# A gated window and dilated attention block: the units' stage keeps projections and attention alone; merges, gating of y and 19 half gate pairs go behind it

## The chip, the cores and the metric

The kernel runs on one core of one Trainium2 chip, as one launch. The metric is device time in microseconds, less is better. The five engines are PE (TensorE, matmul), DVE (VectorE), ACT (ScalarE), POOL (GpSimd) and SP (SyncE, which here issues every DMA). The line numbers L... are those of the kernel before, unless "after" is said.

## What is computed

x is 2048 tokens by 1024 columns. One layer:

```python
h = rms_norm(x, norm_gain)
qa, ka, va, qb, kb, vb, ga, gb, mg = split(h @ w_in)
ya = banded_attention(norm(qa) * s, norm(ka), va, 128, 1, bias, sink) * silu(ga)
for g, (window, dilation) in enumerate(((128, 1), (512, 4), (2048, 16))):
    o, l = dilated_group(norm(qb[g]) * s, norm(kb[g]), vb[g], window, dilation, bias)
yb = sum(softmax(l over the groups) * o) * silu(gb)
gates = sigmoid(mg + b_merge)
x + (gates[0] * (ya @ w_branch_a) + gates[1] * (yb @ w_branch_b)) @ w_out
```

Mixer A has 8 query and 2 key heads of 64, mixer B 8 heads in each of three groups. The gate columns are ga and gb (512 each) and mg (2 x 1024): with 128 columns to a chunk, 8 chunks of ga and gb, and 16 of mg.

## The kernel before

**Precision.** Each operand of a large matmul is split into two f16 parts, hi and lo. A product is three matmuls of a 128 x 128 stationary tile, hi hi, hi lo and lo hi. XH and XL hold the normed x, turned, as f16 parts: 8 chunks of 128 channels by 2048 tokens and 256 more that repeat the first.

**Order.** Every instruction is put out by a planner written by hand: `at(t, f)` puts a step in a heap, `until(t)` puts out those that are due (L390, L396). The times only set the order of the instructions on each engine's own queue; semaphores do the rest. All engines take their queue in order. SP's queue holds all DMAs, also those that wait for data.

**Stages.** (1) x is loaded, normed, turned and split, and the gate chunks 0 and 1 are computed for the four quarters of 512 tokens. (2) The units' stage: 14 units (2 of A, 12 of B, that is four pairs of heads in three groups), each of 8 slots. A slot projects two blocks of 128 tokens to q, k and v (`Pair`, L634): matmul, copy out, norm, split, and a DMA transpose that gives kq, the f16 parts of q and k turned. `Item` (L749) is one block of queries for two heads: logits `s` on PE (L805), maxima on DVE (L820), exp on ACT (L828), split into `p` (ACT L833, DVE L837), a DMA transpose to `pt` (L843), the product with v on PE (L854). An A slot has four items of up to 384 keys, a B slot two of up to 256. For B with dilation 1 or 4 (8 "shifted" units) the key blocks stand half a block off the query blocks, and so q was projected from aligned tokens and k and v from shifted ones: L651 makes 24 matmuls of 128 columns and 24 of 256 there, and 24 of 384 in the other units.

The outputs of A and of group 0 of B stay in SBUF; those of groups 1 and 2 go to DRAM (`zd`, L889) and come back (`zz`, L863). `a_merge` and `b_merge_q` (L945, L978) apply the softmax denominators, in the units' stage. `YPart` (L893) loads a gate chunk (`gtd`), turns y on PE (L916, four transposes each, 32 times), multiplies on DVE (L920), takes the maximum (L925) and stores y to `ytd`. Forty gate steps (`g_step`, L357: 24 matmuls of 512 columns, then tanh on ACT, the gate on DVE, a store) are put into the slots that the table FILLS names (L103), 36 of them in the 112 slots and 4 just behind. Eight more steps (`mg_step`, L1055) follow while the last attention drains.

(3) The gates' stage: the other five pairs of merge chunks. `gate_pair` (L1285) is two steps. `gate_group` (L1382) computes a gate pair for two quarters of the tokens by seven products of half the size in place of eight: 7 x 12 matmuls of 512 columns stand for four steps of 24. It needs sums and differences of blocks of x (`x_sums`, L1328, on DVE and ACT) and of weights (`w_sums`, L1353, on DVE and ACT). Weight pairs are loaded, multiplied by the norm gain on POOL (L180), scaled and split (`prep`, L1305). Before it uses seven products for quarters 0 and 2 of each pair, and steps for quarters 1 and 3.

(4) The branches' stage, `branch_pair` (L1542): y times the branch weights, times the gates; the blocks of the merged result (`a_blocks`, L1497) go to DRAM. (5) The output's stage, `group` (L1618), in seven products for each block.

Of the kernel before, what the change touches and what calls it, by code (L numbers as in the profile page):

```python
# [43 lines left out]
DCS = (3, 1, 5, 0, 4, 2)  # L44
# [16 lines left out]
NPAIR = 8 * NU  # L61

# [7 lines left out]
B_LAST = 0.763  # L70
DRAIN = 0.8
A_MERGE = (0.085, 0.258, 0.51, 0.671, 1.503, 0.761)
B_MERGE = (-0.037, 0.133, 0.333, 0.507, 0.665, 1.053)
Y_PART = (-0.097, 0.483, 0.709, 0.893, 0.943)
GATE = (-0.123, -0.064, 0.329)
W_STEP = (0.1, 0.465, 1.9, 0.445, 4.197, 0.146, 0.342)
W_MAX = (3.762, 3.892)
G_PREP = (5.907, 6.882, 7.102, 7.671, 7.712, 7.812, 7.942)
N_PREP = (6.3, 7.15, 7.753)
B_GAP = (0.25, 0.138, 0.231)  # L80
Y_MAX = (0.026, 0.815, 0.839)
# [8 lines left out]
T_Y = (2.0, 0.8, 1.6, 1.5, 4.0, 26.0, 0.5, 1.3, 2.1, 1.6, 2.0)  # L90
T_P = ((0, 0.0, 0.03), (1, 3.0, 50.0), (2, 56.0, 75.0), (3, 82.0, 102.0), (4, 108.5, 128.3))
T_O = ((0, 62.0, 84.0), (1, 136.4, 154.0), (2, 136.9, 164.6), (3, 183.9, 190.0))
T_G = (143.4, 174.8, 176.0, 177.4)
T_S = (2.0, 11.0, 0.85, 1.6, 0.75, 1.5, 0.9, 1.3, 0.8)
T_H = (157.4, 2.0, 0.02)
T_GATE = (0.1, 0.1, 0.9, 1.0, 1.0)
T_W = (0.3, 5.5, 1.1, 8.5, 0.9, 14.0, 14.7, 16.2, 0.9, 0.8)
T_B = (20.0, 6.5, 1.55, 0.8)
T_BR = (7.0, 0.95, 20.0, 9.0, 34.0)
T_A = (0.3, 0.2, 1.5, 0.8, 1.2)  # L100
T_M = (16.0, 14.0, 2.0, 2.0, 1.0)
# [10 lines left out]
def block_kernel(tc, x, w_units, w_gate, w_mrg, w_brn, w_out, w_bra, gain, qkg, sink, bias_a, bias_b, b_merge, out):  # L112
# [98 lines left out]

    def w_square(u, i):
        raw = wtiles[u][0]
        if i == 0:
            wtiles[u] += [wp.tile([128, NCH, 384], F16, name="wh"), wp.tile([128, NCH, 384], F16, name="wl"),
                          sm.tile([128, 4], F32, name="wsq")]
        n = 384 if u < NU else 256
        c = slice(2 * i, 2 * i + 2)
        A.activation(wtiles[u][2][:, c, :n], raw[:, c, :n], AF.Square, accum_out=wtiles[u][3][:, i:i + 1])
# [12 lines left out]
    def w_hi(u, i):  # L232
        n = 384 if u < NU else 256
        raw, s, inv, wh, wl = wtiles[u]
        c = slice(2 * i, 2 * i + 2)
        A.activation(wh[:, c, :n], raw[:, c, :n], AF.Copy, scale=s[:])
# [43 lines left out]
    zd = [dr.tile([2, S, 132], F32, name=f"zd{p}") for p in range(4)]  # L280
# [32 lines left out]
    gw = {}  # L313
# [12 lines left out]
    def g_square(c):  # L326
        pool = gp if c > 1 else sp0
        bufs = 1 if c > 1 else 2
        gh = pool.tile([128, NCH, 128], F16, name="gh", bufs=bufs)
        gl = pool.tile([128, NCH, 128], F16, name="gl", bufs=bufs)  # L330
# [10 lines left out]
    def g_pow(c):  # L341
# [4 lines left out]
        gw[c] = (gh, gl, ih, raw, s)  # L346

# [190 lines left out]
    for c in range(3):  # L538
        b = X_G[c]
        if c == 2:  # L540
            at(X_G[0] + X_GP[5] + .1, g_load, c)
# [39 lines left out]
    class Unit:  # L581


        def __init__(self, u):
# [13 lines left out]
            self.v, self.kq, self.t, self.done = {}, {}, {}, {}  # L598
            if self.kind == "A" or self.g == 0:
                self.nm = us.tile([128, NT, self.nq], F32, name=f"nm{self.kind}", bufs=2)  # L600
# [33 lines left out]
    class Pair:  # L634
# [7 lines left out]
        def matmuls(self, i):  # L642
# [3 lines left out]
            for a, b, aligned in ((0, 128, True), (128, 384, False)) if un.shift else ((0, 384, True),):  # L646
                h, lo = subset(0, un.g, r, c, aligned), subset(1, un.g, r, c, aligned)
                k = 0
                for ch in range(NCH):
                    for lhs, rhs in ((h, un.wh), (h, un.wl), (lo, un.wh)):  # L650
                        out.append(lambda lhs=lhs, rhs=rhs, ch=ch, a=a, b=b, k=k: T.matmul(  # L651
                            ps[:, a:b], lhsT=lhs[:, ch, :], rhs=rhs[:, ch, a:b], start=(k == 0), stop=(k == 23)))
                        k += 1
# [85 lines left out]
        def turn(self):  # L739
            for i, s in enumerate(self.subsets):  # L740
                if self.un.shift and s[1] == 0:
                    kq = wk.tile([128, 6, 128], F16, name="kq0", bufs=3)
                else:
                    kq = wk.tile([128, 6, 128], F16, name="kq", bufs=KQ_BUFS)
                nc.sync.dma_start_transpose(out=kq[:], in_=self.sp[:, i].rearrange("p a b c -> p (a b c)"))
                self.un.kq[s] = kq


    class Item:  # L749
        def __init__(self, un, r, i, h0):  # L750
# [3 lines left out]
            if un.kind == "A":  # L754
                cs = [c for c in (i - 1, i, i + 1) if 0 <= c < n]
                self.keys = [((0, c), 0, 128) for c in cs]
                self.b0 = 128 * (cs[0] - i + 1)
            elif n == 1:
                cs = [0]
                self.keys = [((r, 0), 0, 128)]  # L760
                self.b0 = 64
            else:
                cs = [i, (i + 1) % n]
                self.keys = [((r, i), 0 if i else 64, 128), ((r, (i + 1) % n), 0, 128 if i + 1 < n else 64)]
                self.b0 = self.p0 = 0 if i else 64
            self.segs = [(r, c) for c in cs]
            self.W = sum(b - a for _, a, b in self.keys)
            self.width = 128 * len(cs)

        def plan(self, s):  # L770
# [5 lines left out]
            if un.kind == "B" and un.g == 0 and self.i % 2 == 0:  # L776
                at(v - .05, self.z_load)
# [12 lines left out]
        def logits(self):  # L790
            un = self.un
            q = un.kq[(self.r, self.i)]
# [954 lines left out]
```

## Time and profile before

| what | us |
|---|---|
| median of 3 runs | 1961.19 (1960.42 to 1961.2) |
| span of the profiled execution, first to last instruction | 1958.6 |
| time around the span, median less span | 2.6 |
| stage 1, x and two gate chunks | 0 to about 70 |
| stages 2 and the drain, units | 70 to about 1466 |
| stage 3, gates | 1466 to about 1604 |
| stage 4, branches | 1604 to about 1810 |
| stage 5, output | 1810 to 1959 |

The profile records no time of its own for the profiled execution outside the span; the 2.6 us are taken as the same for both kernels. A matmul's row has a latency of which most lies beside the next matmul; what PE pays for it is the distance from its start to the next start. On DVE and POOL, too, the next instruction starts before the last has ended, by about 0.08 and 0.01 us. The ends of the stages are read from the chain of work that ended last.

### The profile page before, as it was taken

Reading aid. Unit: us, or ns where it says so; the run is one execution under the profiler, and the core shown is the slowest. Engines: PE = TensorE matmul, PEld = TensorE weight load, DVE = VectorE, ACT = ScalarE, POOL = GpSimd, SP = SyncE. Lnnn points to the kernel's source line nnn. Section 1 sums busy time; section 2 is a strip of 40 time slices with the busy share of each in tenths; the row PEclk is TensorE's granted clock in tenths of the full one; section 3 lists DMA queues with packets and bytes.
Section 4 is the critical chain, followed back from the end, with each engine's and each line's share of the span. In section 5 each row is a group of like instructions: output and inputs, shape, how many; then the busy total and the mean of one; then the engine's idle time right before and its main releaser. Section 6 shows DMA issues by size and latency. Waiting matters only on the chain.

```text
span 1958.6 us, 48091 instructions
## 1 busy us (share of the span) xinstructions
PE 1935.7 (99%) x17606; PEld 1392.0 (71%) x17606; DVE 1377.4 (70%) x3604; ACT 1059.8 (54%) x2415; POOL 956.0 (49%) x2440
## 2 busy tenths in 40 slices
PE   8999999999999999999999999999999999999999
PEld 5567896677788898888989889899544444444444
DVE  6668777888768776667876878767776757876312
ACT  7457656776565566565666655656534545432100
POOL 4254556455546656647566676656511210232533
PEclk8999999999999999999999999999999999999999
DMA  6239987797848596677777776755822346788763
GB/s 250 81 81 168 194 150 159 141 187 141 177 101 184 118 185 126 125 148 164 152 132 154 135 169 126 143 118 118 187 81 85 106 165 195 218 241 268 252 228 145
DMA packets 589773, 308.46 MB, mean 157 GB/s; under 512 B 458080, under 2 KB 527328, under 8 KB 588256
## 3 DMA queue, kind: packets, MB, share of 16 engines
q1 hardware_dynamic: 589536, 305.39, 67.0%
q8 instruction: 137, 2.24, 0.5%
q14 instruction: 100, 0.82, 0.1%
HBM read 129.91 MB, written 65.27 MB: 100 GB/s over the span
## 4 chain that ended last, share of the span: by engine, by line
PE 80%; DVE 6%; POOL 6%; issue 4%; ACT 2%; DMA 2%; SPq 0%; POOLq 0%; DVEq 0%; ACTq 0%
PE pj L651 32%; PE pj L308 14%; PE fps L308 13%; PE fps L1614 7%; PE fps L1409 5%; PE s L805 4%; PE pv L854 4%; POOL rs_t L270 1%; DVE rw L715 1%; POOL rs_t L271 1%; DVE qss L703 1%; POOL rs_t L272 1%; POOL rw L722 1%; POOL rs_y L273 1%; PE pt L916 1%
## 5 line engine op out<-in xcount | busy, mean ns | idle before, releaser
L651 PE MATMUL pj<-wl,XH 128*128 128x128 f16 (+2 forms) x2816 | 715.2, 268 | 0.0
L651 PE MATMUL pj<-wh,XH 128*128 128x128 f16 (+2 forms) x2816 | 708.7, 268 | 4.0 <-DVE vt L691 4.0
L651 PE MATMUL pj<-wh,XL 128*128 128x128 f16 (+2 forms) x2816 | 711.6, 269 | 0.0
L651 PEld LDWEIGHTS <-XH 128*128 128x128 f16 x5632 | 574.6, 113 | 64.7 <-issue 5.8
L651 PEld LDWEIGHTS <-XL 128*128 128x128 f16 x2816 | 318.1, 113 | 26.7 <-issue 0.5
L820 DVE CUSTOM_DVE_ANT_0 pr<-s,b,ubuf 128x256 f32<-128x256 f32 (+3 forms) x512 | 218.6, 464 | 48.6 <-PE s L805 47.0
L270 POOL TENSOR_TENSOR rs_t<-rs_y 128x8 f32<-128x8 f32 (+2 forms) x345 | 105.4, 306 | 207.5 <-DVE rs_y L261 142.7
L837 DVE SCALAR_TENSOR_TENSOR p<-pr,p 128x512 f16<-128x512 f32 (+2 forms) x256 | 185.0, 723 | 21.6 <-ACT p L833 21.1
L308 PEld LDWEIGHTS <-wh 128*128 128x128 f16 x960 | 93.7, 98 | 111.0 <-issue 1.5
L715 DVE TENSOR_TENSOR rw<-rw,qr 128x512 f32<-128x512 f32 (+1 forms) x112 | 111.6, 997 | 86.7 <-POOL vt L678 58.4
L722 POOL TENSOR_TENSOR rw<-rw,g 128x128 f32<-128x128 f32 (+1 forms) x224 | 131.1, 605 | 78.1 <-DVE rw L715 62.1
L833 ACT ACTIVATE p<-pr 128x512 f16<-128x512 f32 (+2 forms) x256 | 159.5, 623 | 7.1 <-issue 0.3
L670 ACT ACTIVATE rw<-pj 128x256 f32<-128x256 f32 (+1 forms) x224 | 86.5, 386 | 134.3 <-PE pj L651 133.4
L737 POOL COPY spl<-spl 128x256 f16<-128x256 f16 (+1 forms) x224 | 93.7, 448 | 127.2 <-DVE spl L732 125.7
L308 PE MATMUL fps<-Y,wh 128*128 128x512 f16 x512 | 152.2, 379 | 0.0
L805 PE MATMUL s<-kq 128*128 128x128 f16 (+1 forms) x1856 | 147.3, 218 | 1.5 <-DMA kq<-spl 1.4
L805 PEld LDWEIGHTS <-kq 128*128 128x128 f16 x2016 | 129.8, 98 | 25.1 <-issue 2.0
L308 PE MATMUL pj<-XH,gh 128*128 128x512 f16 x384 | 145.5, 379 | 0.0
L308 PE MATMUL pj<-XH,gl 128*128 128x512 f16 x384 | 145.5, 379 | 0.0
L308 PE MATMUL pj<-XL,gh 128*128 128x512 f16 x384 | 145.5, 379 | 0.0
L1614 PE MATMUL fps<-wt,M 128*128 128x512 f16 (+1 forms) x684 | 145.2, 375 | 0.0
L728 ACT ACTIVATE spl<-rw 128x512 f16<-128x512 f32 (+1 forms) x112 | 72.1, 644 | 126.2 <-POOL vt L678 87.0
(241 smaller groups left out, 3702.2 us busy)
## 6 DMA issues: line engine op xcount, KB each, us to landing
wraw<-in_w_units_dram SPq DMA_DIRECT2D x56, 384.0 KB, 4.6
mtd<-mm SPq DMA_DIRECT2D x56, 256.0 KB, 3.7
M<-mtd SPq DMA_DIRECT2D x8, 1792.0 KB, 9.5
mgd<-fg SPq DMA_DIRECT2D x39, 256.0 KB, 2.1
zd<-z SPq DMA_DIRECT2D x128, 66.0 KB, 1.9
zz<-zd SPq DMA_DIRECT2D x64, 132.0 KB, 2.9
xt<-in_x_dram SPq DMA_DIRECT2D x16, 512.0 KB, 8.9
gtd<-yo SPq DMA_DIRECT2D x32, 256.0 KB, 2.7
```

Source lines behind the costliest of these rows:

```text
L270: G.tensor_tensor(tv, yv, yv, OP.mult)
L308: out.append(lambda w=w, xx=xx, ch=ch, i=i: T.matmul(ps[:], lhsT=w[:, ch, c0:c0 + 128], rhs=xx[:, ch, ts], start=(i == 0), stop=(i == n - 1)))
L651: out.append(lambda lhs=lhs, rhs=rhs, ch=ch, a=a, b=b, k=k: T.matmul(ps[:, a:b], lhsT=lhs[:, ch, :], rhs=rhs[:, ch, a:b], start=(k == 0), ...
L715: V.tensor_tensor(q, q, self.rr[:, :n].unsqueeze(2).to_broadcast([128, n, HD]), OP.mult)
L722: G.tensor_tensor(q[:, i, :un.nq, :], q[:, i, :un.nq, :], g, OP.mult)
L737: G.tensor_copy(sp[:, i, nh:, :, :], sp[:, i, nq:nh, ::-1, :])
L805: T.matmul(self.sv[j][:, o:o + k1 - k0], lhsT=q[:, h, :], rhs=kt[:, un.nq + kh + v * un.nk, k0:k1], start=(v == 0), stop=(v == 1))
L820: V.tensor_tensor_reduce(out=self.pv[:, j, self.p0:self.p0 + W], in0=self.sv[j], in1=un.bias[:, self.h0 + j, self.b0:self.b0 + W], scale=I ...
L833: A.activation(self.sp[:, :128 * n], self.pr, AF.Copy, scale=PSC)
L837: V.scalar_tensor_tensor(self.sp[:, 128 * n:], self.pr, PSC, self.sp[:, :128 * n], OP.mult, OP.subtract)
L1409: mm.append(lambda ch=ch, k=k, w=w, i=i: T.matmul(ps[:], lhsT=weight(bl, ch)[w], rhs=xblock(x, ch)[k], start=(i == 0), stop=(i == 11)))
L1614: mm.append(lambda ch=ch, k=k, w=w, i=i: T.matmul(ps[:, :cols.stop - cols.start], lhsT=m[:, a, ch, k, :], rhs=wt[w][:, b, ch, cols], start ...
```

## The change

Gate chunks 2 to 7 become three pairs ("s", 2), ("s", 4), ("s", 6), beside the eight merge pairs ("m", ...): 11 pairs of 256 columns. The first runs in eight steps while the attention drains, the second for quarters 1 and 3 in steps, and all else in seven products: 19 halves (a half is a gate pair for two quarters). FILLS is gone, and with it all gate work in the 112 slots. `gate_out` (after L1346) does the tanh and, for "s" pairs, the gate on DVE.

`Pair.matmuls` takes q, k and v from one set of shifted tokens: 24 matmuls of 384 columns for all units. The DMA transposes write into tiles of 512 token columns in token order, at half a block's offset; where a tile begins, a block goes over in two transposes of 64 tokens. `Item.operands` takes q and keys from these tiles, so that a key stretch of up to 256 columns is one matmul.

Every item stores its output to DRAM (`za`, `zd`). `a_merge` runs 8 times and `b_merge_q` 16 times (it was 32, of half the size) in the gates' stage, from DRAM, as does `YPart`; the scales that hang on the maxima of y (`y_scales`) are computed after that. The four sums `whole` in `x_sums` and the four differences in `w_sums` move from DVE to POOL; `x_sums` runs for both pairs of quarters. The splits of the output weights' columns 2 and 3 move into the branches' stage.

```diff
@@ PAIRS
+PAIRS = [("m", dc) for dc in DCS]
+PAIRS[2:2], PAIRS[0:0] = [("s", 4), ("s", 6)], [("s", 2)]
-FILLS = ((2, None, (2, 2, 4, 5)), (3, 0, (8, 9, 10, 12)), (4, 1, (17, 18, 20, 21)), (5, 2, (24, 25, 26, 28)), (6, 3, (32, 35, 37, 38)), (7, 4, (40, 41, 42, 44)), (9, 6, (57, 59, 60, 61)), (10, 7, (64, 65, 66, 68)), (11, 10, (88, 89, 90, 92)), (8, 13, (116, 116, 118, 118)))
-KQ_BUFS = 6
+KQ_BUFS = 3
+Z_BUFS = 9
...
@@ Pair.matmuls
-            for a, b, aligned in ((0, 128, True), (128, 384, False)) if un.shift else ((0, 384, True),):
-                h, lo = subset(0, un.g, r, c, aligned), subset(1, un.g, r, c, aligned)
...
+            h, lo = subset(0, un.g, r, c, not un.shift), subset(1, un.g, r, c, not un.shift)
+            for ch in range(NCH):
+                for lhs, rhs in ((h, un.wh), (h, un.wl), (lo, un.wh)):
+                    out.append(lambda lhs=lhs, rhs=rhs, ch=ch, k=k: T.matmul(
+                        ps[:, :384], lhsT=lhs[:, ch, :], rhs=rhs[:, ch, :384], start=(k == 0), stop=(k == 23)))
@@ Pair.turn (shifted units)
+            for i, (r, c) in enumerate(self.subsets):
+                m, b = divmod(un.n * r + c, 4)
+                if b == 0:
+                    un.kt[m] = wk.tile([128, 3072], F16, name="kq", bufs=KQ_BUFS)[:].rearrange("p (a b) -> p a b", a=6)
...
+                        turned(un.kt[m if c == 0 else m - 1][:, :, 448:512], i, slice(0, 64))
+                    turned(un.kt[m][:, :, 0:64], i, slice(64, 128))
+                else:
+                    turned(un.kt[m][:, :, 128 * b - 64:128 * b + 64], i)
@@ Item.out
+            A.activation(self.z[:, :, 0:65], self.po[:, :, 0:65], AF.Copy)
+            at(T0 + .1, self.z_store)
@@ w_sums
-                at(now[0] + (T_S[3] if n else .72) * k, lambda o=o, x=x, y=y: V.tensor_tensor(o, x, y, OP.subtract))
+                at(now[0] + d * i, lambda o=o, x=x, y=y: G.tensor_tensor(o, x, y, OP.subtract))
@@ x_sums
-            V.tensor_tensor(o, XH[:, ch, tok:tok + 512], XL[:, ch, tok:tok + 512], OP.add)
+            o2 = 512 * p + tok
+            G.tensor_tensor(o, XH[:, ch, o2:o2 + 512], XL[:, ch, o2:o2 + 512], OP.add)
@@ the gates' stage
+    order_ = [("c", 1, 1), ("c", 1, 3), ("s", 1, 0), ("s", 2, 0), ("s", 2, 1)]
+    order_ += [("s", n, p) for n in range(3, 9) for p in range(2)] + [("s", 9, 1), ("s", 10, 1), ("s", 9, 0), ("s", 10, 0)]
...
+    for p in range(2):
+        for c in range(4):
+            at(t + T_X[p] + T_X[2] * c, x_sums, t + T_X[p] + T_X[2] * c, c, p)
+    m = t + T_Z[0]
+    for j in range(2):
+        for q in range(4):
+            at(m, a_merge, m, j, q)
+            m += T_Z[1]
+    for j in range(4):
+        for q in range(4):
+            at(m, b_merge_q, m, j, q)
+            m += T_Z[2]
+    at(m + T_Z[3], y_scales)
```

In `order_`, "c" is a gate pair for one quarter in steps (48 matmuls), "s" a half in seven products (84 matmuls); the second entry is the pair, the third the quarter or the half. T_X is (0.5, 25.538, 5.083), T_Z begins (66.0, 8.5, 10.8), in the planner's microseconds.

More of the change, by code (lines that the diff above doesn't have):

```diff
@@ L893, in block_kernel, with in_turn, __init__ @@
+            nc.sync.dma_start(out=dst, in_=self.z[:].rearrange("p h f -> p (h f)"))
+            done.add(("z", self.un.kind, un.idx, un.g, self.r, self.i, self.h0))
+    def in_turn(t, times, *groups):
+        steps, b = [], 0
+        for d, f in zip(times, [f for g in groups for f in g]):
+            b = max(b, t + d)
+            steps.append((b, *f) if isinstance(f, tuple) else (b, f))
+            b += .001
+        return steps
     class YPart:
-        def __init__(self, chunk, q, y):
-            self.chunk, self.q, self.y = chunk, q, y
+        def __init__(self, chunk, q, y, o):
+            self.chunk, self.q, self.y, self.o = chunk, q, y, o
@@ L1291, in gate_pair @@
+    def gate_pair(n, q):
+        done.add(("conv", q))
         for k in range(2):
             ps = ps_p.tile([128, 512], F32, name="fps")
[L1293 to L1301 removed]
@@ new lines, in block_kernel @@
+    order_ += [("s", n, p) for n in range(3, 9) for p in range(2)] + [("s", 9, 1), ("s", 10, 1), ("s", 9, 0), ("s", 10, 0)]
+    begins, e = {}, t
+    for k, n, p in order_:
+        begins.setdefault(n, e)
+        begins["end", n, p] = e + (10.4 if k == "c" else HALF)
+        e += 10.4 if k == "c" else HALF
+    w_sums(t + .03, 1, (2, 3))
+    ld = t + T_P[0]
+    for n in range(2, 11):
+        late = T_P[4] if n < 4 else 0
+        t2 = max(begins[n - 1] if n > 2 else ld, ld + T_P[1] + late)
+        prep(n, ld, t2, late)
+        w_sums(t2 + T_P[2], n)
+        ld = t2 + T_P[2] + T_P[3]
@@ L1480, in block_kernel @@
+    y_part(e + T_G[3], 0, 2, 0.9)
+    for k, n, p in order_:
+        (gate_pair if k == "c" else gate_group)(n, p)
+    assert abs(clock[0] - e) < 1e-3
     until(clock[0] + T_GATE[4] + .1)
```

565 lines of the change are left out of this document (280 added, 285 removed).

## The prediction

> **What bounds the kernel now.** The first view is the page: busy time, the slices, and the chain that ended last.
>
> ```profile
> PE 1935.7 (99%) x17606; PEld 1392.0 (71%) x17606; DVE 1377.4 (70%) x3604; ACT 1059.8 (54%) x2415; POOL 956.0 (49%) x2440
> ...
> PE   8999999999999999999999999999999999999999
> ...
> DVE  6668777888768776667876878767776757876312
> ...
> POOL 4254556455546656647566676656511210232533
> PEclk8999999999999999999999999999999999999999
> ...
> PE 80%; DVE 6%; POOL 6%; issue 4%; ACT 2%; DMA 2%; SPq 0%; POOLq 0%; DVEq 0%; ACTq 0%
> ```
>
> PE is busy in every slice, at nearly the full granted clock, and the chain is PE's. So a matmul taken away is worth its distance to the next one, unless another engine then falls behind. POOL's slices tell where: up to 7 tenths until about 1400, then 1 or 2, which is the gates' stage (slices 30 to 32). That is where the change puts POOL and DVE work.
>
> The distances come from the timeline, two rows in succession for each form, and from the chain:
>
> ```profile
> 1119.59 0.27 PE L651 MATMUL pj<-wl,XH 128*128 128x256 f16 x1
> 1119.70 0.27 PE L651 MATMUL pj<-wh,XL 128*128 128x256 f16 x1
> ```
> ```profile
> 533.33 0.22 PE L651 MATMUL pj<-wh,XH 128*128 128x128 f16 x1
> 533.38 0.22 PE L651 MATMUL pj<-wl,XH 128*128 128x128 f16 x1
> ```
> ```profile
> 104.24 0.33 PE L651 MATMUL pj<-wl,XH 128*128 128x384 f16 x1
> 104.40 0.33 PE L651 MATMUL pj<-wh,XL 128*128 128x384 f16 x1
> ```
> ```profile
> 505.22 0.45 PE pt L916 x4
> ...
> 512.40 4.00 PE pj L651 x14
> ...
> 1603.06 207.20 PE fps L308 x960
> 1810.26 145.08 PE fps L1614 x684
> ```
>
> 512 columns cost 207.20 / 960 = 0.216 us, 384 some 0.163, 256 some 0.109 and 128 some 0.055 (rows are rounded; I use 0.0555 for the last).
>
> **The change, part by part.**
>
> *Seven products.* Gate work was 8 + 40 + 8 + 20 steps of 24 matmuls and 420 matmuls of seven products: 2244. It becomes 8 + 8 + 4 steps and 19 x 84 = 1596: 2076. The built instruction lists have these counts. So 168 matmuls x 0.216 = **-36.3 us**, certain as work, wherever it runs.
>
> *q, k and v from one set of tokens.* 8 shifted units x 16 blocks x 24 = 3072 times 0.0555 + 0.109 - 0.163: **-5 us**, 0 to -7 by the rounding. Fewer, wider logits matmuls: 1 us more, so **-6**. The 36 more transposes (260 for 224) take SP 1.22 us each, some 3 to a slot, and those of a shifted unit land in the two slots that they had before.
>
> ```profile
> 591.73 1.22 SPq L745 DMA_TRANSPOSE kq<-spl  x1
> ```
> ```profile
> zd<-z SPq DMA_DIRECT2D x128, 66.0 KB, 1.9
> ...
> pt<-p SPq DMA_TRANSPOSE x256, 3.6
> ...
> kq<-spl SPq DMA_TRANSPOSE x224, 2.9
> ```
>
> *The units' stage.* Without fills a B slot is as those were that had none. From 720 to 780 and 960 to 1100 they run at the pace of PE, with merges in them. The stalls of this stage show beside three windows (first column the stretch, second its length, then PE, PEld, DVE, ACT and POOL busy, granted clock):
>
> ```profile
> 172.20:185.40 13.20, 13.20 (x184) 10.28 (x183) 11.87 (x36) 12.32 (x27) 8.41 (x19) 1.00 0.90 153
> 505.10:519.90 14.80, 11.81 (x88) 9.11 (x87) 9.28 (x35) 8.94 (x22) 6.21 (x21) 0.88 0.83 214
> 880.00:920.00 40.00, 40.00 (x446) 33.30 (x444) 32.21 (x99) 21.46 (x54) 29.18 (x75) 1.00 0.75 168
> 1119.20:1131.70 12.50, 9.81 (x112) 8.78 (x109) 10.81 (x38) 9.76 (x24) 8.98 (x25) 0.86 0.64 145
> 1367.30:1379.80 12.50, 11.33 (x126) 8.81 (x124) 10.85 (x38) 7.62 (x19) 9.02 (x25) 1.00 0.48 103
> ```
>
> At 505 PE waits 3.0 us (14.80 less 11.81) behind a gate load of YPart, and then 14 matmuls take 4.00 us where 14 x 0.163 = 2.3 would do. At 1119 it waits 2.7 us behind a DVE that does merges. At 1367 1.2. By the matmuls in these stretches at full pace the losses are 5.6, 4.9 and 2.2 us; their causes, YPart, merges and gate preparation, leave the stage: **-12.7**, at least -5 if something else is late next.
>
> *A slots.* An A slot without fill is the first window: 13.2 us with PE busy all the time, ACT 12.3 and DVE 11.9. Until now about half of the slots with A items had a fill of 5.2 us of PE beside them. Without, some 17 slots stand close together, each with PE's 13.2, ACT and DVE a little below it, and on SP's queue six transposes of 1.22 us and four stores. I take **+5**, some 0.3 for each slot. The bounds: 0, if the queues even it out as they did in that window, and +25, if each slot takes 1.5 more than now.
>
> *The gates' stage* grows on PE by the gate work that the units' stage loses, and 32 x 4 turns of y go with it (0.45 us for four in the chain above, the same there as here: 32 x 0.45 = 14). Loads and stores of merges, 56 loads, 32 of gates and 32 stores of y, go to an SP queue that has room. PE needs the 96 + 1596 matmuls that stand behind the units in the new list (1692 x 0.216 = 366) and these turns, 380 us. The new load is on DVE and POOL, and these two hold each other up. The timeline of the branches' stage shows it, ahead of it the durations alone:
>
> ```profile
> 1657.85 0.74 DVE L1178 SCALAR_TENSOR_TENSOR Y<-yq,ubuf,Y 128x512 f16<-128x512 f32 x1
> 1658.51 0.74 DVE L1178 SCALAR_TENSOR_TENSOR Y<-yg,ubuf,Y 128x512 f16<-128x512 f32 x1
> ```
> ```profile
> 1664.12 1.27 POOL L1557 TENSOR_TENSOR kp<-kp,fg 128x512 f32<-128x512 f32 x1 [2.48 <-DVE fg L1550]
> ```
> ```profile
> 1654.90 2.43 DVE L1178 SCALAR_TENSOR_TENSOR Y<-yq,ubuf,Y 128x512 f16<-128x512 f32 x2
> ```
> ```profile
> 1655.20 1.57 POOL L1557 TENSOR_TENSOR kp<-kp,fg 128x512 f32<-128x512 f32 x1 [55.17 <-DMA fg<-mgd]
> ```
>
> Alone a split with two inputs from SBUF takes DVE 0.66 us (start to start), a sum takes POOL 1.27. Together, two splits and a sum take 2.43 us; one after the other they would take 0.66 + 1.27 + 0.66 = 2.59. So they share by turns: 94% of the sum. Operations of DVE that read PSUM (L1550) don't. The Trainium skill ("SBUF — State Buffer", Who interferes with whom) has the rule: a DVE instruction with two SBUF inputs and a reading GpSimd instruction hold a shared read port in turns, whole instructions long. The trace agrees, but for the 6%.
>
> What a stage needs of this pair, at durations alone:
>
> ```profile
> L1010 POOL TENSOR_TENSOR zz<-zz,bm_e 128x256 f32<-128x256 f32 x96 | 77.0, 829 | 28.1 <-DVE bm_e L1005 28.1
> ...
> L180 POOL TENSOR_TENSOR wraw<-wraw,gn 128x512 f32<-128x512 f32 x24 | 28.2, 1191 | 43.1 <-DMA wraw<-in_w_mrg_dram 43.1
> L970 POOL TENSOR_TENSOR ya<-zz,am_e 128x512 f32<-128x512 f32 x16 | 18.2, 1135 | 3.5 <-DVE am_e L965 3.5
> ```
> ```profile
> L399 DVE TENSOR_TENSOR Y<-Y 128x512 f32<-128x512 f32 x16 | 11.8, 737 | 0.1
> L1341 DVE SCALAR_TENSOR_TENSOR wt<-Y,wt 128x512 f16<-128x512 f32 x16 | 11.7, 735 | 1.5 <-ACT wt L1337 1.5
> L1334 DVE TENSOR_TENSOR Y<-XH,XL 128x512 f32<-128x512 f16 x16 | 11.5, 735 | 0.0
> ```
>
> POOL: 110 sums (32 of x, 40 of weights, 38 of products) at 1.27, 36 gains, 48 and 16 merge products at some 1.05 (below the means, which hold waits): 245 us. That POOL adds f16 at 1.27 no row shows; a copy of half as many f16 takes it 0.4, so 0.8 is the lower bound, 15 us less. DVE: some 170 splits and 70 sums with two SBUF inputs at 0.66 and 0.61, plus small ones: 160. Together 405, by turns 380 us, as much as PE's 380.
>
> It isn't even. The third product (of sums S1) of the fifth entry in `order_` (pair 2, second half) needs nearly all of `x_sums`: 32 x 1.27 + 32 x 0.61 + 32 x 0.66 = 81 us, and with it the weights of pairs 1 and 2, four gains of pair 3 and four sums of products, some 27: 108, by turns 102. PE comes there after two entries of 10.4, two of 18.2 and 7.1 of the fifth: 64 us. A few splits may follow later, so PE is late by **+34**, in two steps (some 14 us in the first half of pair 1, the rest here). Of the 380 us by turns 102 are done by then, and 280 remain beside 316 of PE, a load of 88%; the stretch 880 to 920 in the fence above has about that and PE waits none. I add +5 for waits in the chain of load, products, turn and gate (0 to 25), and +4 for the clock: two long stalls at some 2 us each (5.6 - 3.0 = 2.6 at 505). The Trainium skill ("TensorE: Matmul & The Clock Gate", The HAM clock gate) gives the rule behind: an idle window of some 3.4 us halves the clock. Here 3.0 were enough. **+43** for this stage, 0 to 85.
>
> *Branches.* 14 splits and 6 sums more, some 13 us of DVE in 206 in which it was busy 151; eight PSUM banks of 2.6 us cover them: 0, at most +5.
>
> ```profile
> 1604.00:1810.00 206.00, 206.00 (x956) 93.43 (x955) 150.86 (x224) 84.02 (x133) 42.69 (x31) 1.00 0.73 227
> ```
>
> **The sum:** 1958.6 - 36.3 - 6 - 12.7 + 5 + 43 = 1951.6, with 2.6 us around the span 1954.2. I say **1954**, against a median of 1961.2.
>
> **Rivals.** (1) *The turns stay hidden.* The splits that PE needs come early enough, or f16 sums cost 0.8: the stage loses 0 to 20 us. For it: two-input operations waited in the units' stage all along, and PE did not. Against: 108 us of work is due at 64. Time: 1961.2 - 36.3 - 6 - 12.7 + 5 + 12 = 1923.
>
> (2) *The pair of DVE and POOL sets the whole stage.* Slower than before. If by turns the sum holds in full (405) and a tenth is lost to waits in the queues (a DVE instruction that waits holds up the copies out of PSUM behind it; POOL's products wait for loads of 3 us), the stage takes 450 us, not 380: 1961.2 - 36.3 - 6 - 12.7 + 5 + 70 and 10 for the clock, 1991. It decides from a loss of 55 us on, where the gain is used up. For it: each merge is a chain SP, DVE, ACT, DVE, POOL, DVE, PE, and the turn stands on PE's queue ahead of products.
>
> The rule of the Trainium skill ("SBUF — State Buffer", Who interferes with whom), taken by itself, has whole instructions in turn and no 6% off, which is this rival's 405.
>
> (3) *A slots are set by DVE, ACT and SP.* At 15.5 us in 17 slots they lose 2.3 x 17 = 39 us in place of 5: 1954 + 34 = 1988. Against: the window at 172 is 13.2.
>
> That the matmuls don't go isn't possible, since the lists count them.
>
> **How the numbers follow.** A measurement of this kernel tells about 0.2% (3.9 us) from no change. Near the forecast but clearly faster, 1938 to 1957: 0.32. The same with some more loss, 1957.3 to 1965.1: 0.14. Rival 1: 0.20. Rival 2: 0.24. Rival 3: 0.10. So faster 0.52, same 0.14, slower 0.34. The range reaches to both sides, 1918 to 1991; the forecast's own is 1938 to 1965.
>
> **What would show it.** Right: in the gates' stage PE waits for `x_sums` (releaser DVE, or ACT behind it) some 14 and 20 us in its first 100 us, with POOL and DVE busy in turn there; POOL sums of 1.8 us and more; no stall of 3 us at units 3 and 10; A slots near 13 us; matmuls of 384 columns at 0.163. Wrong: PE waits under 10 us in those first 100 us (rival 1), waits spread over the whole stage with `fps` released by DVE (rival 2), or A slots over 14 us (rival 3).

## The result, and the profile after

The changed kernel takes **2059.9 us** (median of 4, 2057.5 to 2062.4) for 1960.8: a ratio of 1.051 (1.050 to 1.053). It is slower. The forecast of 1954 was wrong, and the time lies above its range, which ended at 1991.

The page of the changed kernel:

```profile
PE 1922.8 (93%) x13700; PEld 1202.9 (58%) x13700; DVE 1488.7 (72%) x3478; ACT 1099.2 (53%) x2493; POOL 1084.6 (53%) x2460
...
PE   8989999999999999999999997778889899999999
...
DVE  6588769867677677667776657978888877787522
...
POOL 4254565556656656656665636755566541123434
PEclk9999999999999999999999999889999999999999
DMA  5269779975876786866775661145556555779764
```

PE has fallen from 99% to 93% of the span, and its slices show where: 7 tenths in slices 25 to 27 and 8 in the three behind them, from 1236 to 1545, in the gates' stage. There the clock is 8 in two slices, DVE is at 7 to 9 and POOL at 5 to 7, where POOL was at 1 or 2 in the gates' stage before. The stages, each from its first matmul to the first of the next one, in both kernels (so the gates' stage before starts earlier here than in the table further up, and the branches' later):

| stage | before | after | forecast's step |
|---|---|---|---|
| x | 70 | 70 | no change |
| units with the drain | 1379, with 48 gate steps | 1181, with 8 | stalls -12.7, A slots +5 |
| gates | 195 | 483 | 380 of PE and 43 lost |
| branches | 166 | 178 | no loss |
| output | 149 | 149 | no change |

The stages hold different work in the two kernels, so what counts is how far each lies above its matmuls at full pace. In the gates' stage those are 1692 x 0.216 + 14 = 379 us, as forecast, and it takes 483: **104 lost, not 43**. PE is busy for 408 us of the 483, so 75 of the 104 are waits, and 29 are matmuls below full pace behind them: after the wait of 4.8 us that ends at 1445, matmuls of 512 columns follow each other at 0.43 us for some 5 us, in place of 0.216. What PE waited for in that stage (total us, times, longest):

```profile
PE fps L199 <- ACT XL L228: 27.3, 4, 16.4
PE fps L939 <- DVE wt L1048: 16.3, 6, 5.0
PE fps L939 <- POOL wt L1005: 13.0, 6, 4.8
PE fps L199 <- DVE ym L957: 6.3, 3, 2.3
PE fps L1441 <- DVE yq L1104: 4.3, 1, 4.3
```

L199 is a matmul of one column that adds up squares over partitions, for the scale of a pair of weights (`w_sum`) or of a chunk of y; L939 is the turn of y. These stand in PE's queue ahead of products; L1441 is a product itself. The five rows are 67 us; seven smaller ones make up the rest. In the units' stage PE waits at other places than before; first the kernel before, then after:

```profile
PE pj L651 <- DVE vt L691: 4.0, 4, 2.4
PE pt L194 <- DVE yo L920: 3.0, 1, 3.0
PE s L805 <- DMA kq<-spl: 1.4, 3, 0.8
```
```profile
PE s L825 <- DMA kq<-spl: 16.3, 16, 2.1
PE pv L894 <- DMA pt<-p: 15.2, 14, 2.1
PE s L825 <- DVE z L860: 5.2, 8, 0.9
PE pj L657 <- DVE vt L697: 3.4, 6, 1.8
```

The rows of after come to 40 us, those of before to 8. So two stages have to be explained, and the gates' stage is the larger.

### The profile page after: what moved, and what is told of

Same layout as the page of the kernel before. It is cut to its first block, busy times and chain, and to the rows that moved or that the text cites. A ratio compares the mean times of both kernels' runs of the same rounds, so it can differ in the third digit from the quotient of the medians.

```text
span 2060.6 us, 40879 instructions
## 1 busy us (share of the span) xinstructions
PE 1922.8 (93%) x13700; PEld 1202.9 (58%) x13700; DVE 1488.7 (72%) x3478; ACT 1099.2 (53%) x2493; POOL 1084.6 (53%) x2460
## 5 line engine op out<-in xcount | busy, mean ns | idle before, releaser
L657 PE MATMUL pj<-wh,XH 128*128 128x384 f16 x1792 | 585.2, 327 | 3.6 <-DVE vt L697 3.4
L657 PE MATMUL pj<-wh,XL 128*128 128x384 f16 x1792 | 586.5, 327 | 0.0
L657 PE MATMUL pj<-wl,XH 128*128 128x384 f16 x1792 | 585.0, 326 | 0.0
L657 PEld LDWEIGHTS <-XH 128*128 128x128 f16 x3584 | 411.9, 116 | 148.1 <-issue 5.8
L868 ACT ACTIVATE pr<-pr,z 128x256 f32<-128x256 f32 (+3 forms) x512 | 226.2, 494 | 37.2 <-DVE z L860 37.0
L657 PEld LDWEIGHTS <-XL 128*128 128x128 f16 x1792 | 207.5, 116 | 64.2 <-issue 0.3
L825 PE MATMUL s<-kq 128*128 128x256 f16 (+3 forms) x1328 | 149.6, 243 | 21.6 <-DMA kq<-spl 16.3
L894 PEld LDWEIGHTS <-pt 128*128 128x128 f16 x3024 | 124.1, 97 | 49.7 <-DMA pt<-p 22.2
L894 PE MATMUL pv<-vt,pt 128*128 128x65 f16 (+1 forms) x2784 | 132.0, 193 | 15.3 <-DMA pt<-p 15.2
L825 PEld LDWEIGHTS <-kq 128*128 128x128 f16 x1328 | 109.8, 98 | 59.5 <-DMA kq<-spl 17.4
L185 POOL TENSOR_TENSOR wraw<-wraw,gn 128x768 f32<-128x768 f32 (+1 forms) x100 | 136.6, 1374 | 0.3 <-DMA wraw<-in_w_mrg_dram 0.3
L1441 PEld LDWEIGHTS <-wh 128*128 128x128 f16 x760 | 76.9, 102 | 91.2 <-issue 11.0
```

The lines of the kernel that those rows point to most:

```text
L185: G.tensor_tensor(v, v, gn[:, c0:c0 + 2].unsqueeze(2).to_broadcast([128, 2, n]), OP.mult)
L657: out.append(lambda lhs=lhs, rhs=rhs, ch=ch, k=k: T.matmul(ps[:, :384], lhsT=lhs[:, ch, :], rhs=rhs[:, ch, :384], start=(k == 0), stop=(k ...
L825: T.matmul(self.sv[j][:, o:o + w], lhsT=q[0][:, h, q[1]:q[1] + 128], rhs=kt[:, kh + v * un.nk, k0:k0 + w], start=(v == 0), stop=(v == 1))
L868: A.activation(v, v, AF.Exp, bias=self.stat(j), scale=-1.0)
L894: T.matmul(self.po[:, j, :w], lhsT=p[:, n * j + s, :], rhs=un.v[key][:, vh, c0:c0 + w], start=(k == 0 and s == 0), stop=(k == 2 and s == n ...
L1441: mm.append(lambda ch=ch, k=k, w=w, i=i: T.matmul(ps[:], lhsT=weight(bl, ch)[w], rhs=xblock(x, ch, p)[k], start=(i == 0), stop=(i == 11)))
```

## The experiments

**First four.** E1 moves the sums of x back to DVE:

```
 def whole(o, ch, tok):
-    G.tensor_tensor(o, XH[...], XL[...], OP.add)
+    V.tensor_tensor(o, XH[...], XL[...], OP.add)
```

> The 32 sums of hi and lo in x_sums go from POOL to DVE, nothing else. Theory A, turns between DVE and POOL: in the changed kernel x_sums ran from 1255 to 1348, with POOL at 1.57 us for a sum that takes it 1.27 alone, and DVE at some 1.56 for each two-input operation that takes it 0.61 to 0.66 alone, one of DVE for one of POOL. On DVE alone the 96 operations are 96 x 0.63 = 60 us, and POOL's gains come through at once. PE's waits of 10.2 and 16.4 us go down to a few: 20 to 35 us less, 2025 to 2040. Theory B, DVE itself is the bound there: 32 more operations on it cost 20 us, and the time is the same or up to 20 longer (2060 to 2080).

2052.9 us, ratio to before 1.047 (1.044 to 1.049): 7 us less than the change. The waits at L199 went from 10.2 and 16.4 us to 2.6 and 14.2. Neither theory's number: the gates' stage got 11 us shorter (471.5 for 482.9), not 20 to 35.

E2 takes from the turn of y what it waits for:

```
-    T.transpose(self.ps[...], self.y[:, b, :], idf[:])
+    T.transpose(self.ps[...], idf[:], idf[:])
```

> The 128 transposes of y in the gates' stage read the identity matrix, which has long been there, and not the merged y: y is left out of the result, all else is done as before. Theory A, the turn stands ahead of products on PE's queue and is put out before its merge is done: PE's waits of some 34 us at the turns go, and with them what the clock loses behind them: 40 to 55 us less, some 2010. Theory B, DVE and POOL can't do more in this time whatever PE waits for: the waits come back at other rows (products that wait for weights or banks), and the gain is under 15 us, 2045 to 2060.

2060.0 us, ratio 1.050 (1.049 to 1.052): nothing gained. No row of L939 is left, and the other waits have grown by as much:

```profile
PE fps L199 <- ACT XL L228: 41.2, 5, 16.4
PE fps L199 <- DVE ym L957: 27.2, 6, 9.1
```

So the turn's wait for its data isn't the cause. PE is late because something else is, and waits at whatever it comes to first.

E3 and E4 are on the A slots of the units' stage. E3 turns half of p by DMA and takes the hi half in place of lo in the product, so lo is left out of the result; E4 spares DVE the lo half but turns the hi half twice.

```
 E3 +  if A: dma_start_transpose(out=pt[:, :n], in_=sp[:, :128 * n]); ph = pl = pt[:, :n]
 E4 +  if A: two of these, into pt[:, :n] and pt[:, n:]; no V.scalar_tensor_tensor for lo
```

> In units of A the transpose of p turns the hi half alone, and the hi half stands for the lo half in the product with v (lo is left out of the result, DVE still computes it). Theory A, the DMA engines are the bound in slots of A: they are 0.87 to 1.0 busy in slots 5 to 11 and 21 to 27, which take 13.7 us in the mean where PE needs 12.0. Half of the p transposes away takes them to some 0.7, and these slots go to the 12.5 us of PE: 20 to 30 us less, 2030 to 2040. Theory B, DVE (0.93) and ACT (0.85) or the length of the chain of an item set the slot: under 8 us less, 2052 to 2060.

> In units of A DVE doesn't compute the lo half of p; the hi half is turned twice instead, in two transposes of half the size, so that the DMA engines move as much as before (lo is left out of the result). Theory A, the DMA engines are the bound in slots of A: no gain, 2055 to 2070, since the second issue costs SP some 1 us for each item. Theory B, DVE is the bound there: four operations of 0.9 us less in each slot, 15 to 25 us less in all, 2035 to 2045.

E3: 2045.6 us, 1.043 (1.041 to 1.044), 14 less, between its two theories. E4: 2102.1 us, 1.072 (1.070 to 1.073), 42 *more*, though DVE had less to do; that is outside the ranges of both theories. A stretch of A slots after the change, then of E3 and of E4 (length, then PE, PEld, DVE, ACT and POOL busy, clock, DMA share, GB/s):

```profile
131.30:230.00 98.70, 89.82 (x1035) 65.94 (x1033) 84.84 (x204) 75.03 (x163) 47.94 (x133) 0.98 0.95 174
```
```profile
131.30:222.00 90.70, 88.94 (x1048) 67.55 (x1046) 84.02 (x204) 75.83 (x166) 50.94 (x131) 1.00 0.74 132
```
```profile
145.90:230.00 84.10, 70.28 (x737) 49.72 (x735) 39.05 (x120) 53.27 (x116) 27.55 (x94) 0.94 0.81 150
```

In E4 the DMA engines are *less* busy (0.81 for 0.95), DVE is at less than half, and PE waits more. What more there is, is issues: 64 more transposes (320 of p for 256). So the number of issues counts, and that is SP's queue. It has issues in 113 of the 119 us from 131 to 250 in E4, in 90 of the 99 from 131 to 230 after the change, and in the kernel before, in A slots without za stores, in 33 of the 51 from 134 to 185. Its timeline after the change, over about one such slot:

```profile
186.51 0.38 SPq L908 DMA_DIRECT2D za<-z  x1
187.00 2.26 SPq L883 DMA_TRANSPOSE pt<-p  x1
189.31 0.57 SPq L180 DMA_DIRECT2D wraw<-in_w_units_dram  x1
189.97 0.38 SPq L908 DMA_DIRECT2D za<-z  x1
190.46 2.32 SPq L883 DMA_TRANSPOSE pt<-p  x1
192.87 0.54 SPq L908 DMA_DIRECT2D za<-z  x1
193.50 2.54 SPq L749 DMA_TRANSPOSE kq<-spl  x2
196.15 1.44 SPq L883 DMA_TRANSPOSE pt<-p  x1
197.68 0.87 SPq L908 DMA_DIRECT2D za<-z  x1
198.66 1.28 SPq L883 DMA_TRANSPOSE pt<-p  x1
200.03 0.98 SPq L908 DMA_DIRECT2D za<-z  x1
```

From 186.5 to 201.0 its rows leave gaps of about a tenth of a us. The issue of a transpose of p takes 1.3 to 2.3 us here, and after each comes a store of za that the kernel before does not have. From 131 to 230 a transpose of p takes SP 1.72 us in the mean. In E3, with half the size and the DMA engines at 0.74, it takes 1.31: so the load of the DMA engines or the size enters by the length of the issue, which these runs don't tell apart.

**Second group.** E5 puts two outputs into one tile and one store:

```
-    self.z = wk.tile([128, 2, 66], F32, name="z", bufs=9)
+    if k == 0: un.zz = wk.tile([128, 2, 2, 66], F32, name="z", bufs=5)
+    self.z = un.zz[:, k]
+    if k == 1: at(T0 + .1, self.z_store)
```

> The outputs of two items, which follow each other, lie in one tile and go to DRAM by one DMA: 128 stores of z for 256, the same bytes, nothing else changed. Theory A, SP's time to issue is the bound in slots of A: SP is 94% busy from 131 to 230 in the changed kernel, 47 us of it with 27 transposes of p, 19 with 15 of kq, and 20 with 28 stores of za, which the kernel before doesn't have there (A's outputs stayed in SBUF). 14 stores less in this stretch are 10 us, about the same in the other one, and slots of A go to 12.5 to 13 us: 12 to 25 us less, 2035 to 2048. Theory B, the transposes in the DMA engines set these slots, whoever issues: under 5 us less.

2049.4 us, 1.046 (1.043 to 1.048): some 10 less, a little under theory A's 12. The same stretch, and the waits of PE in the stage:

```profile
130.70:222.00 91.30, 87.56 (x1037) 66.12 (x1035) 82.98 (x204) 74.85 (x164) 51.14 (x132) 1.00 0.97 191
```
```profile
PE s L825 <- DMA kq<-spl: 14.4, 14, 3.2
...
PE pv L898 <- DMA pt<-p: 5.3, 6, 1.3
```

The waits for p fell from 15.2 us to 5.3 with the same bytes moved (191 GB/s, more than before the edit): it was the issues. The waits for kq hardly fell.

E6 puts the merges' and the gating's steps out later:

```
-A_MERGE = (4.588, 5.306, 7.494, 7.578, 10.432, 1.944)
+A_MERGE = (6.5, 7.5, 10.0, 10.2, 13.0, 4.9)
-B_MERGE = (4.5, 5.692, 7.721, 9.584, 10.41, 10.858, 13.0, 2.546)
+B_MERGE = (7.0, 8.5, 11.5, 14.0, 15.5, 17.0, 20.0, 8.5)
-T_Z = (..., 11.961, 4.431)
+T_Z = (..., 28.0, 11.5)
```

> The steps of the merges and of the gating of y are put out later against their own loads (the exponents 2 to 2.5 us, products and sums 3 to 7, turn, gate and store 3 to 6 after that); no work is added or taken. Theory A, the planner puts these steps into the in-order queues of DVE, POOL and PE before their data are there: in the gates' stage DVE waits some 20 us for loads of zd and gtd and PE 34 at the turns, and what stands behind waits with them. Then the waits go and the stage gets 25 to 50 us shorter, 2010 to 2035. Theory B, DVE and POOL have too much to do in this stage: the same waits come up at other rows, under 12 us less.

2062.6 us, 1.053 (1.051 to 1.054): nothing, theory B. With E2 this speaks against the place of the merges and turns in the queues as the cause; other orders weren't tried.

E7 leaves POOL's work out of the gates' stage, but for the gains:

```
 whole:     A.activation(o, XH[...], AF.Copy)
 w_sums:    no G.tensor_tensor(o, x, y, OP.subtract)
 add:       return
 products:  a_merge A.activation(y, z, AF.Copy); b_merge none
```

> In the gates' stage POOL keeps the gains alone: the sums of x are copies of hi on ACT, products of a_merge are copies on ACT, and the differences of weights, the products of b_merge and the sums of products on POOL are left out (the result is not the reference's). DVE, PE and SP have the work that they had. Theory A, POOL and DVE hold each other up: DVE's 207 us on the chain of this stage hold some 240 operations of 0.61 to 0.66 us that take 1.0 to 1.6 while POOL works. Then the stage comes near to PE's 380 us: 60 to 90 us less, 1970 to 2000. Theory B, DVE's own work, the loads of the merges and the order of the queues set the stage: 10 to 30 us less, 2030 to 2050.

1972.7 us, 1.007 (1.005 to 1.009): **87 less**, theory A. The gates' stage after the change and in E7:

```profile
1251.00:1734.00 483.00, 408.22 (x1854) 188.81 (x1855) 410.98 (x773) 191.44 (x353) 273.34 (x206) 0.93 0.46 147
```
```profile
1248.00:1648.30 400.30, 387.06 (x1854) 184.99 (x1855) 319.33 (x774) 213.26 (x403) 42.13 (x36) 0.99 0.56 178
```

DVE executes the same 773 operations or so in both, and is busy 411 us in the one and 319 in the other. POOL is busy 273 us in the one and 42 in the other.

**Third group.** Is it POOL's mere work beside DVE, or the way of the data through POOL? E9 is E7 with sums on POOL whose result nobody needs; E8 and E10 compute all, with less on POOL.

```
 E9   def beside(): G.tensor_tensor(scr, scr, scr, OP.add)
 E10  products: 8 x A.activation(zv[:, b, h], zv[:, b, h], AF.Copy, scale=e[:, g, b, h]) for each of POOL;
      gains of pairs 1 to 10: 2 x A.activation(v, v, AF.Copy, scale=gn[:, c]); stores in pairs
 E8   as E10, and whole, w_sums and add on V instead of G
```

> As the run that left POOL's work out, but POOL executes a sum of 128 x 512 f32 on a tile of its own at each place where work was left out in the gates' stage; nothing waits for these sums, and they wait for nothing (the same parts of the computation are left out). Theory A, reading by POOL holds up DVE's two-input operations whoever needs the result: DVE's busy time in the stage goes from 317 back to 370 or more, and 1973 becomes 2005 to 2045. Theory B, the way through POOL costs (results that come late, waits in its queue): 1971 to 1985.

> The whole of the computation, with the stores of z in pairs, and in the gates' stage no work on POOL but the gains of the first two pairs: the sums of x, the differences of weights and the sums of products are on DVE, the products of the merges are 8 operations of ACT for each of POOL, the other gains 2 of ACT for each. Theory A, the turns with POOL are what DVE loses: without POOL DVE was busy 317 us in this stage, and 110 operations of 0.62 us more make 385, beside 379 of PE. The stage takes 400 to 415 us in place of 483, and with 10 us from the stores the time is 1970 to 1990. Theory B, DVE is as full as before and the longer chains through ACT take the rest: 2015 to 2050.

> The whole of the computation, with the stores of z in pairs; in the gates' stage the products of the merges and the gains of pairs 2 to 10 go from POOL to ACT (8 and 2 operations for each), the sums of x, the differences of weights and the sums of products stay on POOL. That takes 64 + 36 of POOL's 206 operations, some 105 of 273 us. Theory A, the turns: the loss of 104 us goes down by 30 to 45%, with the stores 2005 to 2025. Theory B, ACT's long rows of small operations hold up its copies out of PSUM: 2040 to 2060.

E9: 2032.9 us, 1.038 (1.036 to 1.040). 60 of the 87 us come back by POOL's mere work, theory A. ACT does the same in E7 and E9, and DVE executes as many operations, in 396 us for 319:

```profile
1247.50:1707.10 459.60, 402.20 (x1854) 187.58 (x1855) 395.99 (x773) 214.65 (x403) 242.93 (x208) 0.94 0.49 155
```

POOL's gains stand behind these sums in its queue and could be late for that alone. But of the 59 us that PE waits in this stage of E9, DVE is busy in 54. The other 27 us of the 87 aren't taken apart: E9's sums are 31 us less of POOL than the change has, and nothing waits for them.

E8: 2055.2 us, 1.048 (1.046 to 1.050). E10: 2080.6, 1.061 (1.060 to 1.063), slower than the change. Both are above theory B's range too, so neither theory's number came. E10's row shows a reason:

```profile
1238.70:1752.50 513.80, 423.56 (x1854) 191.45 (x1855) 374.37 (x771) 337.10 (x937) 153.75 (x106) 0.91 0.43 138
```

ACT went from 191 us to 337 and from 353 instructions to 937. DVE is down to 374, yet the stage is longer: ACT's rows of 8 small products stand ahead of its copies out of PSUM. While PE waits in this stage of E10 (88 us), ACT is busy for 67 and DVE for 59. E8 is like it, with POOL at nothing, DVE at 370 and ACT at 337 in a stage of 491 us. So these two say little of the turns; they say that the stage can be lost on ACT as well.

E11 and E12 split E7: E11 leaves out the products of the merges alone, E12 all the rest.

> Of POOL's work in the gates' stage the products of the merges alone are left out: 48 of b_merge not done, 16 of a_merge a copy on ACT (the result is not the reference's). The sums of x, the differences of weights, the sums of products and the gains stay on POOL. Theory A, each POOL operation costs the stage in the measure of its time: the products are 73 of the 230 us that the run without POOL's work left out, and that run gained 87: some 28 us less, 2025 to 2040. Theory B, the stage is lost at its begin, where x_sums stands on POOL, and the merges come late only because of that: under 12 us less. Theory C, the chains of the merges are what costs: 50 us or more less.

> The other part of the run without POOL's work: in the gates' stage the sums of x are copies of hi on ACT, the differences of weights and the sums of products on POOL are left out; the products of the merges and the gains stay on POOL (the result is not the reference's). Theory A, as for the run before: 157 of 230 us of POOL, some 59 us less, 1995 to 2010. Theory B, the begin of the stage with x_sums is all: 75 us less or more, 1975 to 1985. Theory C, the chains of the merges cost most: 30 to 40 us less, the 40 us lost up to 1364 alone, 2020 to 2030.

E11: 2043.1 us, 1.044 (1.042 to 1.045), 17 less. E12: 1988.7, 1.015 (1.013 to 1.017), 71 less. Together 88, which is E7. Each lies between its theories A and B: the sums of x, weights and products cost 4 times the merges' products, though they are only twice POOL's time. The stage in E11 and in E12:

```profile
1249.80:1715.80 466.00, 402.20 (x1854) 186.30 (x1855) 392.99 (x771) 198.05 (x369) 197.12 (x142) 0.95 0.48 152
```
```profile
1249.00:1663.30 414.30, 392.14 (x1854) 185.14 (x1855) 336.58 (x772) 205.48 (x387) 115.99 (x100) 0.98 0.54 172
```

E13 computes all, with the sums of E12 on DVE, products and gains on POOL, stores in pairs. E14 takes both causes out (E7, E5 and E3 in one).

```
 whole, w_sums, add:  G.tensor_tensor -> V.tensor_tensor
```

> The whole of the computation, with the stores of z in pairs. In the gates' stage the sums of x, the differences of weights and the sums of products are on DVE, 110 operations of some 0.62 us; products of merges and gains stay on POOL (100 operations, some 115 us). Leaving these 110 out gained 68 us in this stage. Theory A, it is POOL's reading beside DVE that costs: most of that stays, less the 68 us that DVE now does itself in so far as it is full: the stage some 440 us for 483, and with 10 us from the stores 2005 to 2020. Theory B, DVE is full either way, whoever holds it up: the stage 465 to 490, 2035 to 2055.

> Both causes taken out together: the run without POOL's work in the gates' stage (sums of x as copies of hi, differences, products of b_merge and sums of products left out), with the stores of z in pairs, and in units of A half of the transposes of p (lo left out of the result). Theory A, the two causes are all that the forecast missed, and they don't meet: 2060 - 87 - 10 and 5 to 10 more for the transposes, 1952 to 1964, which is the forecast's 1954. Theory B, the stage of the units is then held by something else (the begin of a unit of A, loads of weights): 1966 to 1975.

E13: 2027.1 us, 1.034 (1.032 to 1.036), the best that computes all, still slower than before. It lies between the theories:

```profile
1239.60:1702.50 462.90, 404.84 (x1854) 187.94 (x1855) 401.44 (x878) 192.11 (x353) 118.27 (x100) 0.95 0.48 153
```

POOL's time is down by 155 us, yet DVE is as busy as before (401), now with 878 operations of its own: 20 us of the stage come back, not 68. E14: 1965.8, 1.003 (1.002 to 1.005), at the edge of theory B.

**What follows.** In the runs that left ACT's work about as it was, the gates' stage goes with the time that DVE is busy: 319, 337, 393, 396, 401 and 411 us of DVE give 400, 414, 466, 460, 463 and 483 of stage (E7, E12, E11, E9, E13, the change), DVE at 80 to 87%. And while PE waits, DVE works: of PE's 76 us of waits in this stage after the change DVE is busy in 68, ACT in 31, POOL in 53; in E13 of 59.5 DVE in 54, POOL in 14.5. So DVE is the bound, in order and with waits of its own, hence not at 100%. That is read from these rows; what E9 shows by itself is that POOL's work beside DVE costs 60 of the 87 us. With its own 319 us DVE would just fit beside PE's 379; POOL's work adds 92. Put on DVE instead, POOL's sums add nearly as much by themselves (401 in E13 for 337 in E12).

## Why the prediction was wrong

**The step that failed** is the one on the pair of DVE and POOL: "DVE: some 170 splits and 70 sums with two SBUF inputs [...] 160. Together 405, by turns 380 us, as much as PE's 380." It counted of DVE only what shares with POOL. DVE's other work in this stage, nearly as large again, was left out, as if it ran elsewhere: 93 sums out of PSUM alone are 63 us,

```profile
L1449 DVE SCALAR_TENSOR_TENSOR fg<-fps,fg 128x512 f32<-128x512 f32 x93 | 63.0, 682 | 13.0 <-PE fps L1441 6.0 <-POOL fg L1452 4.8 <-DMA Y<-in_w_out_dram 2.2
```

and the gating of y, its maxima and the small steps of the merges make up the rest of 319 (E7). The right sum is 319 + what POOL holds up = 411 of DVE's queue, beside 379 of PE. So DVE's queue alone is longer than PE's work. The forecast's comparison, the stretch 880 to 920 in which PE waited none, has DVE busy for 32 of 40 us, 80%; here it is 108% of PE's 379. Rival 2 came nearest, with PE's waits spread over the whole stage as it said, but by this sum and not by its "405 and a tenth": it had +80 for the stage where 104 came.

**The turns themselves** were right in kind. In x_sums three splits on DVE and the operations on POOL in the same time, each in a fence of its own:

```profile
1274.92 4.64 DVE L1413 SCALAR_TENSOR_TENSOR wt<-Y,wt 128x512 f16<-128x512 f32 x3
```
```profile
1274.41 1.60 POOL L1406 TENSOR_TENSOR Y<-XH,XL 128x512 f32<-128x512 f16 x1
1275.97 1.48 POOL L185 TENSOR_TENSOR wraw<-wraw,gn 128x512 f32<-128x512 f32 x1
1277.42 1.59 POOL L1406 TENSOR_TENSOR Y<-XH,XL 128x512 f32<-128x512 f16 x1
```

One of DVE for one of POOL. From start to start the sum of x on POOL takes 1.56 us (its duration was 1.57 in the forecast's own fence), with a split in it: 0.66 + 1.27 alone would be 1.93, so 81% of the sum, less than the 94% of the forecast. But for DVE the price isn't a share. A split that takes 0.66 takes 1.55, and a step of a merge that is hardly work at all can wait for a whole operation of POOL. First two such steps with POOL idle, then two beside two operations of POOL, each ending when one of these ends:

```profile
1427.64 0.16 DVE L997 TENSOR_TENSOR am_sd<-Y,am_e 128x16 f32<-128x16 f32 x1
1427.90 0.17 DVE L998 TENSOR_TENSOR am_sd<-am_sd,am_f 128x16 f32<-128x16 f32 x1
```
```profile
1440.42 1.23 DVE L997 TENSOR_TENSOR am_sd<-Y,am_e 128x16 f32<-128x16 f32 x1
1441.76 1.23 DVE L998 TENSOR_TENSOR am_sd<-am_sd,am_f 128x16 f32<-128x16 f32 x1
```
```profile
1439.91 3.05 POOL L1109 TENSOR_TENSOR wraw<-wraw 128x512 f32<-128x512 f32 x2
```

0.16 us became 1.23. Not every operation pays that much: the splits of L253 went from 746 ns in the mean in E7 to 1065 after the change. E9 shows that the price needs no dependence: POOL at work on a tile of its own is enough (its sums read and write; which of the two counts wasn't tried). The Trainium skill ("SBUF — State Buffer", Who interferes with whom) says that a DVE instruction with two SBUF inputs contends with a GpSimd instruction that reads SBUF, and calls the shared port pair "an exclusive lock". The 1.23 us of a step of 0.16 agree with it; the 81% shows that a part of an instruction does lie beside the other's.

**x_sums** at the begin: forecast +34 in two steps of some 14 and 20, found 10.2, 4.3 and 16.4, 31 in all. The place was another: PE stood at L199, the sum of squares of weights. Its squares are on ACT behind x_sums' copies, and those wait for DVE; in both long waits DVE is busy from end to end. With POOL's sums of x done by DVE (E1) the two waits are still 2.6 and 14.2. The sign of the forecast, sums of x of 1.8 us and more on POOL, did not come: 1.55 in the mean.

**The chain of merges**, +5 (0 to 25), and +4 for the clock: some 70 us were lost behind the begin. This is mostly the same cause, not the chains: with the turns' data ready (E2) or the steps later (E6) nothing changed, with POOL's work gone (E7) all but 21 of the 104 went. The clock is in this, too: 0.93 after the change, 0.99 in E7, with PE busy 408 us for the work that takes 387 there; the forecast had 4 for it, and 29 came.

**A slots**, +5 (0 to 25), by "six transposes of 1.22 us and four stores" on SP. The count was right, the price was not: from 131 to 230 a slot has on SP four transposes of p at 1.72 us in the mean, two of kq at 1.25 and four stores at 0.70, 12.2 us, where six at 1.22 are 7.3. The 1.22 was read from one transpose of kq in a slot of B. In the kernel before, p's transposes in A slots took 1.53 us in the mean already (134 to 185). These seven slots took 14.2 us in the mean, with PE busy for 12.9 of it, which is rival 3's sign. Before, PE's waits in this stage were 8 us, 7 of them in the three stalls; now they are 40. Rival 3 was true in part: SP, as E4 and E5 show, and not DVE, whose relief in E4 gained nothing. Before, fills of 5.2 us on PE gave SP more time in about half of these slots; the change removed them and added stores. The forecast's own window at 172 had no za stores in it.

Of the 40 us the waits for kq, 16.3, did not go with the stores (14.4 in E5). Most of them stand in units of B. The five longest, 1.7 to 2.1 us, have three or four loads of weights (branches, output or the next unit) between the transposes on SP in the 14 us before; a run without these loads wasn't tried, and their cause stays open.

**The stalls**, -12.7: held, no wait in the units' stage is over 2.1 us. **Seven products**, -36.3: held as work, 379 us in the stage for 380. **q, k and v**, -6: held. In the last unit, shifted and without fills in both kernels, the first six slots (from first projection to first projection) took 8.73, 8.73, 8.74, 9.21, 9.17 and 9.54 us before and take 8.61, 8.61, 8.61, 9.07, 9.05 and 9.40 now, some 0.13 less each, or 8 us in 64 slots, if the others gain as much. **Branches**, 0: 178 us, some 12 above its matmuls at full pace, 8 of which PE waited for DVE; no run was made for it alone, and in E7 it is 4 less.

**Does it add up?** By the stages of the profiled run of the kernel before, the forecast comes to 1143 us for the units (1379 less 40 steps of 5.2, the turns' 14, 6 and 12.7, and 5 more), 423 for the gates and 166 for the branches. Found were 1181, 483 and 178. So two terms were too small, by 60 in the gates' stage and by some 38 in the units' stage, where PE waits 40 us, and 12 came in the branches' stage, which had none. That is 110, beside a span of 2060.6 for 1951.6. With both causes out (E14) the time is 1966: the gates' stage loses 26 there, 17 less than the 43, while the units lie some 21 and the branches 8 above the forecast.

## What to carry to other kernels

When work moves to where an engine looks idle, add up that engine's whole queue and not only the part of it that meets the new load; and where POOL and DVE share, reckon that a two-input operation of DVE can take as long as one of POOL, however short it is alone (0.16 us became 1.23). Work that "fills" a slow stage also hides its second bound: before it is taken out, look up what each queue, SP's too, needs in a slot without it. And a wait that goes away without the time going down (E2, E6) says that the engine was late for another reason.

## What the runs showed of the hardware that was not expected

- POOL sums on a tile that nobody else uses cost 60 us (E9 against E7): DVE's 32 sums of x went from 759 ns to 1211 in the mean.
- The issue of a DMA transpose isn't of fixed length: 1.24 us in a quiet queue, 1.72 in the mean and up to 2.6 with the DMA engines 95% busy, and two of half the size cost more than one (E4: 42 us for 64 more, with the same bytes; 1.33 us each in the mean).
- Products by a factor for each block and head are dear on ACT: 64 of POOL became 512 activations of 0.33 us, 127 us in all; with 72 gains ACT rose by 146 us (E10).
- A wait of PE under 3 us can cost pace behind it: after the one of 2.6 us at 1666 five matmuls of 512 columns come some 0.43 us apart; after the one of 3.1 us at 1531 none do.
